# Two products that take turns on the tiles of x, a later mean, and other expected waits in a planned mixing stage

## The chip, the core and the metric

The kernel runs on one core of a Trainium2 chip. The metric is the device time of one execution in microseconds (us). Five engines run their own lists of instructions in order and wait for each other by semaphores: TensorE (PE, matmuls; its weight loads are listed as PEld), VectorE (DVE), ScalarE (ACT), GpSimd (POOL) and SyncE (SP, which issues nearly all transfers from HBM).

## The reference, cut to what matters

Two transformer blocks in float32 on 512 tokens of width 1024. The change lies in the first half of the first block. `x` is normalised, multiplied by `w_in`, and the columns of the product go to four groups of heads:

```python
def rms_norm(x, g):
    y = xf * lax.rsqrt(jnp.mean(xf * xf, axis=-1, keepdims=True) + EPS)
    return (y * g.astype(jnp.float32)).astype(x.dtype)

def token_mix(h, w_in, ...):
    p = (h @ w_in).astype(jnp.float32)
    ...                                   # fox attention: q, k, v, forget gates
    qkv = jax.nn.silu(causal_dwconv(gdn_qkv, gdn_conv_w))
    g = (-jnp.exp(gdn_a_log) * jax.nn.softplus(gdn_a + gdn_dt_bias)).transpose(0, 2, 1)
    o_b = gated_delta_chunked(l2norm(q), l2norm(k), v, g, beta)
    ...                                   # hgrn and gla: two more linear attentions
```

Then `x = x + mixed @ w_out`, a gated feed-forward with a convolution, and the second block (a convolution mixer, a feed-forward, latent attention, a feed-forward). Those parts are the same before and after.

## The kernel before, in words

**Products.** Everything is kept transposed, 128 features on the partitions and 512 tokens along the row. A product of `w_in` gives 128 output columns: eight k tiles, and for each three matmuls of 512 columns, because both operands are split in a high and a low part (`h` with `xh`, `h` with `xl`, `l` with `xh`; lines 705 ff., `step`). So a product is 24 matmuls into one bank of PSUM. These are the dense matmuls, `mm<-xh,wh`, `mm<-xl,wh`, `mm<-xh,wl` in the trace. The weights come from HBM into `raw` (ring of 3), ACT makes the high part `wh` (line 111) and DVE the low part `wl` (line 112); `wh` and `wl` are rings of 2, so the third weight tile can be split only when the first product is done with its own.

**The norm is late.** The products use `x` times the gain (`xh` line 173, `xl` line 174) without 1/rms. The sum of squares is made beside them (ACT squares, line 156, DVE adds, line 158, result `z`), one matmul with ones (`gps<-z,ones`) sums over the partitions, and `rsqrt_wide` (lines 131 to 146) makes `rb`, 1/rms. Whatever leaves a product's PSUM bank is multiplied with `rb` on the way, so no bank is freed before `rb` is there.

**What follows a product.** `sm` (small gates) is transposed, then ACT makes a softplus of it (`gtmp`, `gl`: Abs, Exp, Ln of lines 873 to 875 of the kernel before), four small DVE operations make `gg`, and a small matmul `gps<-gg,...` its cumulative sums. `gq`, `gk`, `gv` go through a convolution of four taps on ACT and DVE and a silu on ACT; the silu needs another activation table, which is loaded before it, and the table with Exp and Ln after it (1.28 us each).

**Order.** In this stage PE's order is written by a planner, `conduct`: it keeps a clock that advances with each matmul, three lanes of generators (G: the mean, the small gates, the delta rule `gdn0` and `gdn1`; L: `hg0`, `gla`, `hg1`; F: `fox0`, `fox1`) and the dense products as filler. A generator yields the wait it expects for the other engines (`Y_...`, `LV`, `LA`), and until the clock reaches that, PE's list is filled with dense steps. The tags of PSUM are `mm` (2 banks), `gps`, `lps` and `fps` (2 each). The order on the other engines is set by the compiler's scheduler. `start` issues the first loads and splits, `mean` yields `Y_MEAN`, then emits the matmul with ones.

Of the kernel before, what the change touches and what calls it, by code (L numbers as in the profile page):

```python
# [9 lines left out]
F32 = mybir.dt.float32  # L10
F32R = mybir.dt.float32r
# [4 lines left out]
ALU = mybir.AluOpType  # L16
# [11 lines left out]
class Builder:  # L28
# [19 lines left out]

    lane = {}

    def t(self, shape=(128, S), dt=F32, tag="t", bufs=None, name=None):
# [57 lines left out]
    def split(self, src, h, l, eng=None):  # L109
        nc = self.nc  # L110
        nc.scalar.activation(out=h, in_=src, func=ACTF.Copy)  # L111
        (eng or nc.vector).tensor_tensor(out=l, in0=src, in1=h.bitcast(F32), op=ALU.subtract)  # L112

# [16 lines left out]

    def rsqrt_wide(self, ps, scale, tag, n=S):

        nc = self.nc
        r = self.t(tag="u", bufs=3)[:, :n]
        nc.scalar.activation(out=r, in_=ps, func=ACTF.Ln, scale=scale, bias=self.epsD)
        v = self.t(tag="s", bufs=3)[:, :n]
        nc.scalar.activation(out=r, in_=r, func=ACTF.Exp, scale=-0.5)
        if n < S:
            nc.vector.tensor_scalar(out=v, in0=ps, scalar1=scale, scalar2=EPS, op0=ALU.mult, op1=ALU.add)
        else:  # L140
            nc.scalar.activation(out=v, in_=ps, func=ACTF.Identity, scale=scale, bias=self.epsD)
        nc.vector.tensor_tensor(out=v, in0=v, in1=r, op=ALU.mult)
        nc.vector.scalar_tensor_tensor(out=v, in0=v, scalar=-0.5, in1=r, op0=ALU.mult, op1=ALU.mult)
        out = self.t(tag=tag, bufs=3 if tag == "u" else 1) if tag else v
        nc.vector.scalar_tensor_tensor(out=out, in0=v, scalar=1.5, in1=r, op0=ALU.add, op1=ALU.mult)
        return out
# [505 lines left out]
Y_FIN, Y_FOX, Y_GDN, Y_SM = 8.3, 8.64, 4.0, 5.33  # L652
Y_MEAN = 9.5
C_MEAN = 4.2
C_SILU = 4.8
DUE = 4.78

# [6 lines left out]
class Mix(Mla):  # L664
# [93 lines left out]
    def conduct(self, jobs, lanes):  # L758


        self.clk = fed = 0.0
        started = 0
        self.over, self.beside = {None}, []
        self.there = ready = {}
        self.zs = []
        strands = [None] * len(lanes)
        first, last = jobs.pop(0), []
        self.last = last
        xs = [(k, *x) for k, x in enumerate(self.xs)]
        nxt, dense, held = (first, self.first), [], []  # L770
        early = [self.second]
        outs, parked, row = list(range(KD)), [], None
        while True:
# [13 lines left out]
            if nxt is None:  # L787
                job = next((j for j in jobs if j[1] in self.over), None)
                if job:
                    jobs.remove(job)  # L790
                    nxt = job, early.pop() if early else self.weight(self.a["w_in"], job[0], KD)
                elif not jobs and outs:
                    c = outs.pop(0)
                    nxt = (c, None, None, self.out_post(c)), self.weight(self.a["w_out"], c, KD)
# [29 lines left out]
            taken = [d[2] for d in dense] + [p[2] for p in parked] + ["mm"] * len(held)  # L824
            tag = next((t for t in tags if taken.count(t) < 2), None)
            if nxt and tag and len(dense) + len(held) < 2 and all(d[1][2] is None for d in dense):
                job, ws = nxt
                started += 1
                if started in (3, 4):
                    tag = "fps"  # L830
                dense.append((self.stepped(ws, last if job[2] is None else xs, tag), job, tag))
                nxt = None
                continue
# [202 lines left out]
    def gdn(self, p):  # L1036
# [36 lines left out]
        nc.vector.tensor_tensor(out=nk, in0=ss[:, 8:16], in1=rr[:, 8:16], op=ALU.mult)  # L1073
        yield 0.0
        MT, MR, AT, X, XT = [], [], [], [], []
        for j in range(2):
# [35 lines left out]
            MT.append(mt), MR.append(mr), AT.append(at), XT.append(xt)  # L1112
            yield LV
        nc.gpsimd.tensor_tensor(out=d4(ke), in0=d4(ko), in1=b64(eG), op=ALU.mult)
# [382 lines left out]
    def start(self, gi):  # L1497


        idle = self.psm.tile([128, S], F32, tag="lps", name="lps", bufs=2)  # L1500
        for _ in range(11):
            self.nc.tensor.matmul(out=idle[:, :128], lhsT=self.ones, rhs=self.ones, start=True, stop=True)
        self.x = [self.rt("x") for _ in range(KD)]
        self.first = self.weight(self.a["w_in"], T_SMALL, KD, lambda i: self.load(slice(0, 2)) if i else None)
        self.load(slice(2, KD))
        self.xs = self.norm(gi)
        self.second = self.weight(self.a["w_in"], TILES[ORDER.split()[1][:3]], KD)
        self.acc = self.squares(self.x, self.nc.vector)

    def load(self, ks):  # L1510
        for k in range(KD)[ks]:
            self.nc.sync.dma_start(out=self.x[k], in_=self.a["xT"][k])

    def mean(self):

        yield Y_MEAN
        ps = self.pst()
        self.mm(ps, self.ones, self.acc)
        with self.tc.high_priority():
            self.r = self.rsqrt_wide(ps, 1.0 / D, "rb")  # L1520

# [178 lines left out]
```

## Time and profile before

| | us |
|---|---|
| median of 3 runs (1855.84 to 1869.3) | 1856.73 |
| the profiled execution | 1857.77 |
| its span in the trace | 1856.0 |
| PE busy in the span | 1820.7 (98%) |
| DVE, ACT, POOL busy | 1053.8, 737.1, 197.2 |
| PE on the chain that ended last | 86% |

The trace is of the profiled execution; its clock and the run's differ by 1.77 us around the span. Read the share of PE first: where an engine is busy 98% of the time, what is left to look for is the stretches in which it is idle, or in which the granted clock (PEclk) is half of full speed. Then look for what ended each idle time. The names in the rows are those of the program's tiles; "out<-in".

### The profile page before, as it was taken

The page shows a single profiled execution, that of the slowest core. Times are in us where ns is not written, and L with a number is a line of the kernel's source. Part 1 is how long each engine was busy: PE and PEld are TensorE (multiplying, and loading weights), DVE is VectorE, ACT ScalarE, POOL GpSimd, SP SyncE. Part 2 cuts the span into 40 slices and gives each one's busy share as a digit, 9 for nine tenths or more (in the row PEclk, how much of TensorE's full clock was granted, in tenths as well). Part 3 has the DMA queues.
Part 4 walks back from the last instruction along what each step waited for, and adds up shares of the span by engine and source line. Part 5 has one row for each costly group of instructions (what it writes and reads, how often), then busy time and mean ns, then how long its engine had stood idle before and what let it go on. Part 6 is the DMA issues. An engine that isn't in the chain of part 4 may idle for free.

```text
span 1856.0 us, 22094 instructions
## 1 busy us (share of the span) xinstructions
PE 1820.7 (98%) x8631; PEld 1504.2 (81%) x8631; DVE 1053.8 (57%) x1622; ACT 737.1 (40%) x1138; POOL 197.2 (11%) x230
## 2 busy tenths in 40 slices
PE   9999999999999999999999999999999999999997
PEld 6788888778888888888888888888787888888886
DVE  7885976767777633455564444333876454444323
ACT  6543535554444422322342323323577333232322
POOL 2411402210000001111200000010011200000001
PEclk9999999999999999999999999999999999999999
DMA  5111111323222333232323232333212232323332
GB/s 177 48 35 47 46 35 35 120 88 102 92 101 96 92 94 99 97 102 91 103 96 101 93 98 96 94 95 101 69 57 75 80 102 92 103 91 100 94 94 77
DMA packets 53223, 162.61 MB, mean 88 GB/s; under 512 B 6528, under 2 KB 13184, under 8 KB 53120
## 3 DMA queue, kind: packets, MB, share of 16 engines
q1 hardware_dynamic: 52992, 161.21, 27.3%
q8 instruction: 67, 1.10, 0.2%
q14 instruction: 36, 0.29, 0.1%
q10 hardware_dynamic: 128, 0.01, 0.0%
HBM read 157.78 MB, written 2.10 MB: 86 GB/s over the span
## 4 chain that ended last, share of the span: by engine, by line
PE 86%; DVE 8%; ACT 3%; issue 1%; POOL 1%; DMA 0%; DVEq 0%; SPq 0%; POOLq 0%; ACTq 0%
PE mm L125 24%; PE mm L127 24%; PE mm L126 24%; PE mm L705 7%; PE gps L705 3%; PE lps L705 2%; PE fps L705 1%; DVE lbd L1317 1%; DVE wl L112 1%; DVE lat L1368 1%; ACT wh L111 1%; PE ps L577 0%; DVE ptl L112 0%; PE ps L165 0%; DVE nm L580 0%
## 5 line engine op out<-in xcount | busy, mean ns | idle before, releaser
L111 ACT ACTIVATE wh<-raw 128x1024 fp32r<-128x1024 f32 (+3 forms) x308 | 308.6, 1003 | 768.5 <-PE mm L126 459.1
L125 PE MATMUL mm<-xh,wh 128*128 128x512 f32 x1336 | 521.8, 391 | 0.5 <-ACT xh L173 0.5
L126 PE MATMUL mm<-xl,wh 128*128 128x512 f32 x1336 | 520.7, 390 | 0.5 <-DVE xl L174 0.5
L127 PE MATMUL mm<-xh,wl 128*128 128x512 f32 x1336 | 519.9, 389 | 0.0
L112 DVE TENSOR_TENSOR wl<-raw,wh 128x1024 fp32r<-128x1024 f32 (+3 forms) x300 | 362.9, 1210 | 225.6 <-ACT wh L111 222.7
L126 PEld LDWEIGHTS mm<-xl,wh 128*128 128x128 f32 x1336 | 250.8, 188 | 54.5 <-DVE xl L174 1.4
L125 PEld LDWEIGHTS mm<-xh,wh 128*128 128x128 f32 x1336 | 250.8, 188 | 53.8 <-issue 1.0
L127 PEld LDWEIGHTS mm<-xh,wl 128*128 128x128 f32 x1336 | 250.8, 188 | 52.1 <-issue 0.2
L125 PE MATMUL mm<-hidh,wh 128*128 128x512 f32 (+1 forms) x614 | 236.7, 386 | 0.0
L127 PE MATMUL mm<-hidh,wl 128*128 128x512 f32 (+1 forms) x614 | 235.3, 384 | 0.0
L126 PE MATMUL mm<-hidl,wh 128*128 128x512 f32 (+1 forms) x614 | 233.8, 381 | 0.0
L127 PEld LDWEIGHTS mm<-hidh,wl 128*128 128x128 f32 x614 | 115.4, 188 | 24.4
L126 PEld LDWEIGHTS mm<-hidl,wh 128*128 128x128 f32 x614 | 115.4, 188 | 23.6
L125 PEld LDWEIGHTS mm<-hidh,wh 128*128 128x128 f32 x614 | 115.5, 188 | 21.7 <-ACT wh L111 0.2
L705 PE MATMUL mm<-xh,wh 128*128 128x512 f32 x291 | 126.8, 436 | 0.5 <-ACT xh L173 0.4
L705 PE MATMUL mm<-xl,wh 128*128 128x512 f32 x291 | 115.4, 397 | 1.6 <-DVE xl L174 1.3
L705 PE MATMUL mm<-xh,wl 128*128 128x512 f32 x291 | 115.3, 396 | 1.5 <-DVE wl L112 1.5
L278 DVE TENSOR_TENSOR u<-mm,rb 128x512 f32<-128x512 f32 x44 | 30.4, 691 | 141.0 <-PE mm L127 141.0
L158 POOL TENSOR_TENSOR z<-z,sq 128x512 f32<-128x512 f32 x31 | 50.4, 1625 | 557.2 <-ACT sq L156 519.5
L274 DVE TENSOR_TENSOR u<-mm,rb 128x512 f32<-128x512 f32 x44 | 30.4, 691 | 90.9 <-PE mm L127 90.9
L111 ACT ACTIVATE hidh<-s 128x512 fp32r<-128x512 f32 x66 | 41.7, 632 | 88.4 <-DVE s L255 57.5
L215 DVE TENSOR_TENSOR x<-x,mm 128x512 f32<-128x512 f32 x32 | 22.0, 687 | 84.2 <-PE mm L127 84.2
(436 smaller groups left out, 2131.6 us busy)
## 6 DMA issues: line engine op xcount, KB each, us to landing
raw<-in_w_a_dram SPq DMA_DIRECT2D x52, 512.0 KB, 3.3
raw<-in_w_b_dram SPq DMA_DIRECT2D x52, 512.0 KB, 3.3
raw<-in_w_up_dram SPq DMA_DIRECT2D x44, 512.0 KB, 3.3
raw<-in_w_in_dram SPq DMA_DIRECT2D x28, 512.0 KB, 3.3
raw<-in_conv_w_in_dram SPq DMA_DIRECT2D x24, 512.0 KB, 3.3
raw<-in_w_down_dram SPq DMA_DIRECT2D x16, 448.0 KB, 3.4
raw<-in_w_a_dram SPq DMA_DIRECT2D x16, 448.0 KB, 3.4
raw<-in_w_b_dram SPq DMA_DIRECT2D x16, 448.0 KB, 3.4
```

What stands on the lines that cost most here:

```text
L111: nc.scalar.activation(out=h, in_=src, func=ACTF.Copy)
L112: (eng or nc.vector).tensor_tensor(out=l, in0=src, in1=h.bitcast(F32), op=ALU.subtract)
L125: nc.tensor.matmul(out=ps, lhsT=h, rhs=xh, start=(k == 0), stop=False)
L126: nc.tensor.matmul(out=ps, lhsT=h, rhs=xl, start=False, stop=False)
L127: nc.tensor.matmul(out=ps, lhsT=l, rhs=xh, start=False, stop=(k == kt - 1))
L158: eng.tensor_tensor(out=acc, in0=acc, in1=sq, op=ALU.add)
L215: self.nc.vector.tensor_tensor(out=self.x[c], in0=self.x[c], in1=ps, op=ALU.add)
L274: nc.vector.tensor_tensor(out=g, in0=ps, in1=r, op=ALU.mult)
L278: nc.vector.tensor_tensor(out=g, in0=ps, in1=r, op=ALU.mult)
L705: self.nc.tensor.matmul(out=out, lhsT=lhsT, rhs=rhs, start=start, stop=stop)
L1317: nc.vector.tensor_tensor(out=bd[rows, :, h].rearrange("p c (n j) -> p c n j", j=b), in0=c4(q)[rows], in1=c4(d)[rows], op=ALU.mult)
L1368: nc.vector.copy_predicated(out=at.rearrange("p c (n j) -> p c n j", j=2 * b)[:, :, :, b:], mask=self.lmask[:, lv - 1].rearrange("p (n j) ...
```

## The change

1. `start`: the first weight tiles of the first two products (`sm` and `gq`) are loaded and split in halves, with x's tiles between them. The two products then take turns: after two k tiles of the first and two of the second, each further tile of x is used by both before the next. Before, the first product ran alone, its weights in two halves, and the second product's weights came as one tile.
2. `conduct`: the third and fourth product go to the `fps` banks, and before the mean four products may stand in PSUM (`room`). `Y_MEAN` is 12.3 and counts from the end of the first two products; before it was 9.5 from the start.
3. `rsqrt_wide(..., short=True)` for this mean: the product with 1/D and the addition of EPS go from ACT to DVE, and the next weight tile's low part on DVE is held back until `rb` is made.
4. The delta rule: `Y_ROW` = 2.66 instead of 0 before the decay rows, and 2.5 LV instead of LV after the first of the two heads.

```diff
     def split(self, src, h, l, eng=None):
         nc = self.nc
         nc.scalar.activation(out=h, in_=src, func=ACTF.Copy)
-        (eng or nc.vector).tensor_tensor(out=l, in0=src, in1=h.bitcast(F32), op=ALU.subtract)
+        with ExitStack() as order:
+            if self.first_low is not None:
+                order.enter_context(self.tc.issue_after(self.first_low))
+                self.first_low = None
+            (eng or nc.vector).tensor_tensor(out=l, in0=src, in1=h.bitcast(F32), op=ALU.subtract)
...
-        if n < S:
+        if n < S or short:
             nc.vector.tensor_scalar(out=v, in0=ps, scalar1=scale, scalar2=EPS, op0=ALU.mult, op1=ALU.add)
         else:
             nc.scalar.activation(out=v, in_=ps, func=ACTF.Identity, scale=scale, bias=self.epsD)
...
-        nc.vector.scalar_tensor_tensor(out=out, in0=v, scalar=1.5, in1=r, op0=ALU.add, op1=ALU.mult)
+        i = nc.vector.scalar_tensor_tensor(out=out, in0=v, scalar=1.5, in1=r, op0=ALU.add, op1=ALU.mult)
+        if short:
+            self.first_low = i.ins
...
-Y_MEAN = 9.5
-C_MEAN = 4.2
+Y_MEAN = 12.3
+C_MEAN = 4.0
 C_SILU = 4.8
+Y_ROW = 2.66
...
-        started = 0
+        started = 2
...
-        first, last = jobs.pop(0), []
+        last = []
...
-        nxt, dense, held = (first, self.first), [], []
-        early = [self.second]
+        nxt, dense, held = None, [], []
+
+        two = [(self.stepped(ws, xs, "mm"), jobs.pop(0)) for ws in self.firsts]
+        for i in (0, 0, 1, 1, *(0, 1) * (KD - 2)):
+            ps, k = next(two[i][0])
+            if k == KD - 1:
+                held.append((ps, *two[i][1][2:]))
...
-            tag = next((t for t in tags if taken.count(t) < 2), None)
-            if nxt and tag and len(dense) + len(held) < 2 and all(d[1][2] is None for d in dense):
+            tag = "fps" if started in (2, 3) else next((t for t in tags if taken.count(t) < 2), None)
+            room = 2 if "mean" in self.over else 4
+            if nxt and tag and len(dense) + len(held) < room and all(d[1][2] is None for d in dense):
                 job, ws = nxt
                 started += 1
-                if started in (3, 4):
-                    tag = "fps"
...
         nc.vector.tensor_tensor(out=nk, in0=ss[:, 8:16], in1=rr[:, 8:16], op=ALU.mult)
-        yield 0.0
+        yield Y_ROW
...
             MT.append(mt), MR.append(mr), AT.append(at), XT.append(xt)
-            yield LV
+            yield LV if j else 2.5 * LV
...
-        self.first = self.weight(self.a["w_in"], T_SMALL, KD, lambda i: self.load(slice(0, 2)) if i else None)
-        self.load(slice(2, KD))
-        self.xs = self.norm(gi)
-        self.second = self.weight(self.a["w_in"], TILES[ORDER.split()[1][:3]], KD)
+        steps = (("w", 0, 0), ("x", 0), ("x", 1), ("w", 1, 0), ("x", 2), ("x", 3), ("w", 0, 1), ("x", 4),
+                 ("w", 1, 1), ("x", 5), ("x", 6), ("x", 7))
...
         with self.tc.high_priority():
-            self.r = self.rsqrt_wide(ps, 1.0 / D, "rb")
+            self.r = self.rsqrt_wide(ps, 1.0 / D, "rb", short=True)
```

What this does to the lists of instructions is seen at three places. The number behind a tile's name is its buffer.

PE, around the matmul of the mean. Before, in the middle of the second product (`mm_281`, `gq`); the third (`mm_333`, `gk`) goes to another tag's bank:

```order
L705 MATMUL mm_281<-xh_156,wl_167 128x512
L705 MATMUL gps_303<-z_170,ones_77 128x512 [waits DVE_49]
L705 MATMUL mm_281<-xh_160,wh_166 128x512
L705 MATMUL mm_281<-xl_161,wh_166 128x512
L705 MATMUL mm_281<-xh_160,wl_167 128x512
L705 MATMUL mm_333<-xh_132,wh_277 128x512 [waits Activation_49]
L705 MATMUL mm_333<-xl_133,wh_277 128x512
L705 MATMUL mm_333<-xh_132,wl_278 128x512 [waits DVE_49]
```

Now, behind the last matmul of the fourth product (`mm_343`, `gv`); next is the fifth (`mm_415`, `lq`):

```order
L715 MATMUL mm_343<-xl_167,wh_308 128x512
L715 MATMUL mm_343<-xh_166,wl_309 128x512
L715 MATMUL gps_368<-z_170,ones_77 128x512
L715 MATMUL mm_415<-xh_132,wh_339 128x512 [waits DVE_49,Activation_49]
L715 MATMUL mm_415<-xl_133,wh_339 128x512
```

Before, 45 dense matmuls stood ahead of the mean and a product that needs no `rb` behind it; now 96 stand ahead of it, and the product behind it takes the bank of `sm`, so it waits for DVE as well as for ACT.

DVE, from the making of `rb` to what leaves the first two banks. Before (L142, L143, L145 are the three steps to `rb`; L901 takes `sm` out of its bank):

```order
L142 TENSOR_TENSOR u_307<-u_307,u_305 128x512 [waits Activation_49]
L143 SCALAR_TENSOR_TENSOR u_307<-u_307,u_305 128x512 [waits DVE_49]
L112 TENSOR_TENSOR wl_330<-raw_327,wh_329 128x1024 [waits DMAHW5_49,PE_49,Activation_49]
L145 SCALAR_TENSOR_TENSOR rb_312<-u_307,u_305 128x512 [waits DVE_49]
L901 TENSOR_TENSOR sm_314<-mm_250,rb_312 128x512 [waits DVE_49]
```

Now:

```order
L146 TENSOR_SCALAR u_372<-gps_368 128x512 [waits Activation_49]
L149 TENSOR_TENSOR u_372<-u_372,u_370 128x512 [waits DVE_49,Activation_49]
L150 SCALAR_TENSOR_TENSOR u_372<-u_372,u_370 128x512 [waits DVE_49]
L152 SCALAR_TENSOR_TENSOR rb_377<-u_372,u_370 128x512 [waits DVE_49]
L118 TENSOR_TENSOR wl_412<-raw_409,wh_411 128x1024 [waits DMAHW0_49,PE_49]
L915 TENSOR_TENSOR sm_379<-mm_250,rb_377 128x512 [waits DVE_49]
```

The weight split has moved from ahead of the last step to behind it, and still stands ahead of `sm`; a step that ACT did is now the first row.

ACT, around the softplus of the small gates (`gtmp`, `gl`). Before, it stands ahead of all silus:

```order
L226 ACTIVATE gq_322<-z_319,mixp_222 128x512 [waits DVE_49,Pool_49]
L873 ACTIVATE gtmp_375<-gz_371 128x32 [waits DVE_49]
L873 ACTIVATE u_388<-u_387 4x512
L874 ACTIVATE gtmp_375<-gtmp_375 128x32 [waits Activation_49]
L874 ACTIVATE u_388<-u_388 4x512 [waits Activation_49]
L875 ACTIVATE gl_374<-gtmp_375 128x32 [waits Activation_49]
```

Now (line 270 loads the silu's table, line 273 the other; `wh_523` is the weight tile that takes the sixth product's buffer):

```order
L887 ACTIVATE gtmp_453<-gz_449 128x32 [waits DVE_49]
L1452 DMA fk_938<-sm_379 1x16x32 [waits DVE_49]
L888 ACTIVATE gtmp_453<-gtmp_453 128x32 [waits Activation_49]
L113 ACTIVATE wh_523<-raw_521 128x1024 [waits DMAHW2_49,PE_49]
L270 ACT_TABLE_LOAD
L270 ACTIVATE gv_400<-gv_400 128x512 [waits DVE_49]
L270 ACTIVATE gk_392<-gk_392 128x512
L270 ACTIVATE gq_384<-gq_384 128x512
L273 ACT_TABLE_LOAD
L889 ACTIVATE gl_452<-gtmp_453 128x32 [waits Activation_49]
```

The last step, `gl`, has moved behind a weight split that waits for PE, two table loads and three silus. On PE the matmul of `gg`, which needs it, stands three dense matmuls behind the end of the sixth product; the transposes of `gk` and `gq`, which stood 45 dense matmuls behind it, follow at once, and fifteen dense matmuls come between them and the decay rows, where there were none.

## Rows read from the trace of the kernel before

**Rows 1.** The page, busy time of each engine, its share and instructions.

```profile
PE 1820.7 (98%) x8631; PEld 1504.2 (81%) x8631; DVE 1053.8 (57%) x1622; ACT 737.1 (40%) x1138; POOL 197.2 (11%) x230
```

**Rows 2.** PE in order of time: start, length, operation, count, [idle before, releaser].

```profile
6.36 0.49 PE L705 MATMUL mm<-xh,wh 128*128 128x512 f32 x1 [0.25 <-ACT xh L173]
...
9.06 0.40 PE L705 MATMUL mm<-xh,wl 128*128 128x512 f32 x1
...
17.44 0.50 PE L705 MATMUL mm<-xh,wl 128*128 128x512 f32 x1 [1.50 <-DVE wl L112]
...
21.89 1.02 PE L705 MATMUL gps<-z,ones 128*128 128x512 f32 x2
...
36.21 0.40 PE L705 MATMUL mm<-xl,wh 128*128 128x512 f32 x1
...
46.01 0.39 PE L705 MATMUL mm<-xh,wl 128*128 128x512 f32 x1
47.65 0.66 PE L712 MATMUL gps<-mlac,gk 128*128 128x128 f32 x4 [1.25 <-ACT gk L261]
48.17 0.66 PE L712 MATMUL gps<-mlac,gq 128*128 128x128 f32 x4
...
51.65 0.59 PE L705 MATMUL gps<-mixb,identb 128*128 128x512 bf16 x1 [2.82 <-issue]
```

**Rows 3.** Stretches: length, busy time of PE, PEld, DVE, ACT, POOL, granted clock, DMA.

```profile
50.00:51.00 1.00, 0.00 (x0) 0.00 (x0) 0.43 (x1) 1.00 (x4) 0.00 (x0) 0.71 0.00 0
...
57.00:58.00 1.00, 1.00 (x5) 0.77 (x5) 1.00 (x6) 0.59 (x3) 0.03 (x1) 0.88 0.88 291
...
230.00:240.00 10.00, 8.01 (x34) 6.65 (x33) 7.77 (x18) 2.79 (x3) 0.53 (x1) 0.74 0.15 54
240.00:250.00 10.00, 10.00 (x54) 8.70 (x53) 6.21 (x15) 1.06 (x1) 0.53 (x1) 0.92 0.00 0
...
290.00:300.00 10.00, 9.07 (x48) 7.61 (x49) 8.52 (x15) 8.15 (x17) 7.56 (x7) 0.83 0.16 55
```

**Rows 4.** DVE in order of time, 12 to 40 us.

```profile
12.38 2.10 DVE L174 SCALAR_TENSOR_TENSOR xl<-x,gains,xh 128x512 fp32r<-128x512 f32 x3
...
17.31 2.69 DVE L158 TENSOR_TENSOR z<-z,sq 128x512 f32<-128x512 f32 x3
...
26.11 1.22 DVE L112 TENSOR_TENSOR wl<-raw,wh 128x1024 fp32r<-128x1024 f32 x1
...
27.96 0.69 DVE L901 TENSOR_TENSOR sm<-mm,rb 128x512 f32<-128x512 f32 x1
...
38.46 0.74 DVE L228 SCALAR_TENSOR_TENSOR gk<-z,mixp,gk 128x512 f32<-128x512 f32 x1
```

**Rows 5.** ACT in order of time, 20 to 50 us.

```profile
21.10 1.04 ACT L111 ACTIVATE wh<-raw 128x1024 fp32r<-128x1024 f32 x1
22.05 0.19 ACT L1242 ACTIVATE lb<-lb 128x2 f32<-128x2 f32 x1
22.95 0.69 ACT L135 ACTIVATE u<-gps,epsD 128x512 f32<-128x512 f32 x1 [0.72 <-PE gps L705]
...
24.11 0.63 ACT L137 ACTIVATE u<-u 128x512 f32<-128x512 f32 x1
...
46.98 0.61 ACT L261 ACTIVATE gk<-gk 128x512 f32<-128x512 f32 x1
...
48.13 1.28 ACT L264 ACT_TABLE_LOAD   x1
```

**Rows 6.** PE's waits from 50 to 430 us: total, times, longest.

```profile
PE lps L705 <- DVE lst L1408: 2.1, 2, 1.3
PE lps L705 <- DVE gate L1022: 2.0, 1, 2.0
...
PE gps L705 <- DVE gxt L1146: 0.6, 1, 0.6
...
PE gps L705 <- DVE gx L1143: 0.5, 1, 0.5
```

More of the change, by code (lines that the diff above doesn't have):

```diff
@@ L49 @@
     lane = {}
+    first_low = None
     def t(self, shape=(128, S), dt=F32, tag="t", bufs=None, name=None):
@@ L128, in product, with rsqrt_wide @@
         return ps
-    def rsqrt_wide(self, ps, scale, tag, n=S):
+    def rsqrt_wide(self, ps, scale, tag, n=S, short=False):
         nc = self.nc
@@ L790, in conduct @@
                     jobs.remove(job)
-                    nxt = job, early.pop() if early else self.weight(self.a["w_in"], job[0], KD)
+                    nxt = job, self.weight(self.a["w_in"], job[0], KD)
                 elif not jobs and outs:
@@ L1502, in start @@
             self.nc.tensor.matmul(out=idle[:, :128], lhsT=self.ones, rhs=self.ones, start=True, stop=True)
+        nc = self.nc
         self.x = [self.rt("x") for _ in range(KD)]
-        self.first = self.weight(self.a["w_in"], T_SMALL, KD, lambda i: self.load(slice(0, 2)) if i else None)
-        self.load(slice(2, KD))
-        self.xs = self.norm(gi)
-        self.second = self.weight(self.a["w_in"], TILES[ORDER.split()[1][:3]], KD)
[L1508 to L1512, printed above, removed]
+        cts = T_SMALL, TILES[ORDER.split()[1][:3]]
+        raw = [self.raw.tile([128, CHUNK * 128], F32, tag="raw", name="raw") for _ in cts]
+        h = [self.wh.tile([128, CHUNK * 128], F32R, tag="wh", name="wh") for _ in cts]
+        l = [self.wl.tile([128, CHUNK * 128], F32R, tag="wl", name="wl") for _ in cts]
+        steps = (("w", 0, 0), ("x", 0), ("x", 1), ("w", 1, 0), ("x", 2), ("x", 3), ("w", 0, 1), ("x", 4),
+                 ("w", 1, 1), ("x", 5), ("x", 6), ("x", 7))
+        half = lambda i: slice(i * 512, i * 512 + 512)
+        for what, i, *part in steps:
+            if what == "x":
+                nc.sync.dma_start(out=self.x[i], in_=self.a["xT"][i])
+            else:
+                cs = half(part[0])
+                nc.sync.dma_start(out=raw[i][:, cs], in_=self.a["w_in"][cts[i], :, cs])
+        self.xs = []
+        for what, i, *part in steps:
+            if what == "x":
+                self.xs.append(self.gained(self.x[i], self.gain(gi, i), "x"))
+            else:
+                cs = half(part[0])
+                self.split(raw[i][:, cs], h[i][:, cs], l[i][:, cs])
+        col = lambda t, k: t[:, k * 128 : (k + 1) * 128]
+        self.firsts = [[(col(h[i], k), col(l[i], k)) for k in range(KD)] for i in range(2)]
+        self.acc = self.squares(self.x, nc.vector)
     def mean(self):
```

## The prediction

> **What bounds the kernel now.** I read the busy times first: PE is busy 98% of the span [rows 1]. No other engine is over 57%. So the time is PE's list, and a change can win or lose only where PE issues nothing, or runs at half clock. Next I read PE in order of time through the first 60 us, the only place where the change moves whole products, and the granted clock beside it. A dense matmul issues every 0.228 us: 43 of them lie between 36.21 and 46.01 [rows 2]. Everything below counts PE time that is lost against that pace, up to the first `gps<-gq,gk` matmul of the delta rule. What PE has to issue is otherwise the same; the 15 dense matmuls that the change puts ahead of that point are missing later.
>
> Lost before, four pieces. (1) Start: the first dense matmul is at 6.36, the mean's at 21.89, and the 45 between are worth 10.3, so 5.2 lost, 1.5 of it one wait for a weight's low part at 17.44 [rows 2]. (2) From the end of the seventh product (46.01 + 0.23) to the transposes of `gk` at 47.65: 1.4, ended by ACT's silu [rows 2]. (3) From the end of `gq`'s transposes (48.17 + 0.5) to the decay rows at 51.65: 3.0 [rows 2]. (4) Clock: mean 0.71 in 50 to 51 and 0.88 in 57 to 58 [rows 3] put the fall to half speed (1.2 instead of 2.4 GHz) at 50.4 and the return at 57.2; PE works again from 51.65, so 5.6 us at half speed, 2.8 lost. Sum 12.4.
>
> **The change, part by part.**
>
> *Taking turns.* The first six matmuls go as before, since the same three transfers stand ahead of them: they end at 9.06 + 0.23, 2.9 us for 1.4 of work, 1.5 lost [rows 2]. After that each tile of x gives six matmuls, 1.4 us, while DVE needs 0.7 for its low part (three in 2.10) [rows 4] and half as much again for the weight halves. The next 42 should run without a gap, to 18.9. SP's list counts as nothing: 20 transfers of the same bytes stand ahead of the third weight tile in both kernels, and the last three tiles of x come behind the other halves, by at most what PE is behind them anyway. POOL's list doesn't change here.
>
> *The third product.* Both `wh` buffers are now in use until 18.7, so its split can't be early. On ACT it stands behind the three small `lb` steps, which follow DVE's adds of squares. Before, these adds ended at 20.0 (17.31 + 2.69) [rows 4], the third `lb` step began 2.05 later with one 1.04 split between [rows 5], and DVE's work up to there is the same now. At worst the split ends at 22.1, at best, without `lb` ahead, at 19.8. Then two matmuls, and 0.8 more until the low part (1.22) [rows 4] is there. Lost between 1.7 and 4.0; I take 3.4, near the row with `lb` ahead. The early gain is given back here.
>
> *The mean.* Before, the chain from its matmul at 21.89 to `sm` out of its bank at 28.65 took 6.8 us [rows 2, 4], and PE felt nothing: 27 dense matmuls that needed no 1/rms covered it. That is the point: the third product didn't wait for 1/rms before either. Now the mean comes when all four products are done, and the fifth needs `sm`'s bank. The chain itself gets shorter: Ln ended at 23.64 and Exp began at 24.11, and the 0.5 of Identity between goes [rows 5]; the weight split on DVE only moves from ahead of the last step to a place that is still ahead of `sm`, so it saves nothing; ACT has a 1.04 split [rows 5] that starts with the mean's matmul and ends about when Ln may begin, 0.1 more. So 6.4, less 0.5 for the mean's own issue (two passes in 1.02) [rows 2]: 5.9 lost. If that split holds Ln up whole it is 6.9; without the DVE split, 4.8.
>
> *The small gates.* On PE the matmul of `gg` stands three dense matmuls behind the sixth product's end. On ACT the last step to it stands behind `wh_523`, which needs that product's end. From there: split 1.04, table 1.28, three silus 1.7 (the last two took 48.13 - 46.98 = 1.15), table 1.28, Ln 0.2 (as the small `lb` step) [rows 5], four small DVE steps at about the same, partly overlapped, 0.6, and 0.2 for the last matmul to end. That is 6.3, less 0.7 for the three matmuls: 5.6 lost. It holds however early or late the sixth product ends. This rests on ACT not passing a waiting instruction. The trace shows it: `gk`'s last tap ended at 39.2 on DVE [rows 4], and its silu ran at 46.98 [rows 5] behind other work. The Trainium skill, "TensorE: Matmul & The Clock Gate" (Architectural detail), says the same, that ACT and DVE are strict first-in first-out while PE alone may pull weight loads ahead. Were the Ln free to pass, this term and its clock below would go and the sum would end 8.4 lower.
>
> *The waits ahead of the delta rule.* Pieces (2) and (3) of before go: `gk` and `gq` have been through the silu by then, and 15 dense matmuls (3.4 us) cover the 3.0.
>
> *Clock.* Nearly 6 us without a matmul twice; before, 2.0 us idle at 232.7 was enough for a fall. A fall cost 2.8 in (4), and elsewhere 6.8 us at half speed (clock 0.74 and 0.92 in 230 to 250), 3.4 lost, or 3.4 us (0.83 in 290 to 300), 1.7 lost [rows 3]. I take 2.8 each, the row nearest in kind, between 1.7 and 3.4. The skill's same page (What's actually happening) says that the gate's time base runs free of the kernel's start; by that each fall's cost would be drawn anew in each run, anywhere between the two bounds.
>
> *Longer waits later.* What the delta rule itself kept waiting after that point is 0.6 and 0.5 us [rows 6], and the fall of the clock near 290 that follows them, 1.7. The longer expected waits aim at these: 2.8 gained. The other waits are the linear attention's (`lps`), which get no new wait; I leave them.
>
> **Sum.** Lost after: 1.5 + 3.4 + 5.9 + 5.6 + 2 x 2.8 = 22.0; before 12.4; so 9.6 slower there, less 2.8 later: 6.8. The profiled execution took 1857.77, so 1864.6. It lies 1.04 above the median of the runs shown, so **1864** in their terms (1863.5).
>
> **Rivals.**
>
> *Not slower: the later lanes gain more.* The largest wait later is `gate` 2.0 [rows 6] with the fall at 234.7 behind it, 3.4 [rows 3]; DVE is what it waits for, and the second delta rule now no longer runs beside that part of the linear attention. With the two `lst` waits (2.1) [rows 6] gone as well, 7.5 more comes back: 1856. It decides if PE's idle time after 100 us falls below half of before. For it: the change moves work out of that stretch. Against it: the same work then lies beside `hg1`, and waits of one place tend to come back in another. Chance 0.22.
>
> *Slower still.* The wait for the third product's weights is itself long enough for a fall of the clock (2.8 more), and the pattern of the small gates, a weight split that waits for PE with tables and silus behind it, recurs once in front of the second delta rule (5.6): 1872. For it: 2.0 idle was enough once; against it: 1.5 idle at 17.44 was not. Chance 0.15.
>
> *The change doesn't do what its order says.* If the small gates' value is there early enough, or the mean's chain is covered after all, one of the long waits with its clock (8.4) is missing: 1855. Only the places in the lists speak against it, but these are fixed. Chance 0.08.
>
> *The forecast*: two new long waits of PE, 1859 to 1869. Chance 0.55.
>
> **Numbers.** The range for 8 in 10 is 1853 to 1873: the forecast with its bounds, most of the two cheaper cases and the middle of the dearer one. A measurement of this kernel can tell about 1% from no change, 18.6 us. Faster than 1838 would need nearly all of PE's idle time in the stage back: 0.02. Slower than 1875 needs the dear case and more: 0.06. Within 1%: 0.92.
>
> **What would show it.** In PE's list of the changed kernel: a wait of about 3 us for `wh` at the third product; 5 to 7 us between the mean and the fifth product, ended by DVE's `sm`; 5 to 6 us ahead of `gg`, ended by DVE after ACT's second table load; half clock behind each; no wait at the decay rows. The prediction is wrong in its main step if the idle time ahead of the fifth product is under 3 us, wrong in its second if `gg` isn't waited for, and wrong in what is left if the waits after 100 us shrink by more than 6 us or grow.

## The result, and the profile after

The changed kernel takes **1879.3 us** (median of 6 runs, 1877.87 to 1880.63) against 1856.8 before: ratio 1.011, with an interval of 1.0083 to 1.0137. It is slower by 22, where 7 were forecast, and 6 above the end of the range. The profiled execution took 1877.87; its span is 20.1 longer than that of before.

All of it is lost in the stage that the change touches. This is the line of the stage that comes next, the first helper call behind the mixing; its column "first and last start" gives the time at which the next stage begins.

```profile
L131 PE MATMUL mm<-xh,wh x151: 388/390/792, 415.2 to 519.6; 128*128 128x512 f32 x151
```

Before, the same line starts at 395.0, so 20.2 are gone by then; from there to the end both kernels take 1461 us. So each kernel below has two marks: the first `gps<-gq,gk` of the delta rule (60.27 before, 73.80 after), up to which the forecast counted, and this one.

PE in order of time up to the first mark (start, length, operation, idle time before it and what ended it), to be set beside [rows 2]:

```profile
5.95 0.50 PE L715 MATMUL mm<-xh,wh 128*128 128x512 f32 x1 [0.56 <-ACT xh L182]
...
21.33 0.64 PE L715 MATMUL mm<-xh,wh 128*128 128x512 f32 x1 [3.19 <-ACT wh L113]
...
34.26 1.02 PE L715 MATMUL gps<-z,ones 128*128 128x512 f32 x2
40.86 0.77 PE L715 MATMUL mm<-xh,wh 128*128 128x512 f32 x1 [5.58 <-DVE sm L915]
...
60.78 0.61 PE L715 MATMUL gps<-gg,mixc 128*128 128x16 f32 x2 [5.48 <-DVE gg L980]
...
68.04 0.39 PE L715 MATMUL gps<-mixb,identb 128*128 128x512 bf16 x1
...
73.80 1.16 PE L715 MATMUL gps<-gq,gk 64*128 64x128 f32 x8
```

The three waits stand where the forecast put them, and the decay rows (68.04) wait for nothing. Up to here the change costs 73.80 - 60.27, less 15 dense matmuls (3.4) and four small transposes (0.5) that now stand ahead of this point: 9.6.

The other 10.6 come behind it. Between the two marks PE's idle time grew from 9.7 to 17.4, and its time at half clock from 10.2 to 13.7, which is 1.7 lost at most. These are 9.4 of the 10.6; the rest isn't placed. PE's seven largest waits from 80 to 480 us (total, times, longest):

```profile
PE fps L715 <- ACT fpt L1496: 6.4, 2, 4.0
PE mm L715 <- ACT xh L113: 2.3, 2, 1.5
PE gps L722 <- DVE u L1021: 1.9, 1, 1.9
PE gps L715 <- ACT gvn L1191: 1.6, 1, 1.6
PE fps L715 <- ACT sq L1456: 1.3, 1, 1.3
PE lps L715 <- DVE lat L1382: 1.3, 1, 1.3
PE lps L715 <- DVE lst L1422: 0.7, 1, 0.7
```

Against [rows 6]: `gate` (2.0) is gone, `lst` is down from 2.1, and in their place stands `fpt`, the transposed softmax weights of the fox lane, for which no wait is listed before. Stretches with the granted clock (columns as in [rows 3]):

```profile
20.00:30.00 10.00, 8.48 (x30) 6.40 (x31) 2.96 (x7) 3.29 (x5) 0.00 (x0) 0.83 0.33 107
40.00:50.00 10.00, 9.14 (x33) 7.41 (x34) 8.54 (x15) 4.68 (x7) 0.20 (x2) 0.73 0.15 52
60.00:70.00 10.00, 9.21 (x40) 7.94 (x41) 7.32 (x25) 6.96 (x19) 1.05 (x1) 0.70 0.01 2
270.00:280.00 10.00, 6.03 (x29) 4.94 (x28) 5.30 (x17) 6.65 (x16) 0.00 (x0) 0.83 0.16 52
300.00:310.00 10.00, 7.53 (x32) 5.96 (x31) 6.50 (x12) 7.42 (x14) 4.66 (x5) 0.74 0.15 52
310.00:320.00 10.00, 10.00 (x66) 8.78 (x64) 3.42 (x8) 2.29 (x5) 0.00 (x0) 0.92 0.01 2
370.00:380.00 10.00, 8.27 (x38) 6.67 (x37) 4.96 (x9) 3.92 (x7) 0.31 (x1) 0.83 0.43 116
```

A lower clock follows each wait of about 2 us or more: the third product's weights (20:30), the mean, `gg`, both waits on `fpt`, and those on `u` (1.88) and `xh` (1.51) at 370. Why `fpt` is late shows in ACT's list ahead of it, in order of time:

```profile
268.65 1.06 ACT L113 ACTIVATE wh<-raw 128x1024 fp32r<-128x1024 f32 x1
269.73 1.28 ACT L270 ACT_TABLE_LOAD   x1
271.02 1.15 ACT L270 ACTIVATE gate<-gate 128x512 f32<-128x512 f32 x2
272.19 1.28 ACT L273 ACT_TABLE_LOAD   x1
...
274.17 0.27 ACT L1496 ACTIVATE fpt<-fps 128x128 f32<-128x128 f32 x1
```

PE's transpose that fills its bank ran here, and the product that needs the copy here:

```profile
268.78 0.27 PE L722 MATMUL fps<-mlac,fp 128*128 128x128 f32 x1
...
274.49 0.69 PE L715 MATMUL fps<-fv,fpt 128*128 128x64 f32 x2 [3.97 <-ACT fpt L1496]
```

The input is ready at 269.05, 0.4 after ACT has begun a weight split. ACT then does split, table load, two silus and table load, 4.8 us, and three small steps, 0.7, before it gets to a copy of 0.27. The second wait has the same pattern ahead of it, with one silu:

```profile
300.37 1.04 ACT L113 ACTIVATE wh<-raw 128x1024 fp32r<-128x1024 f32 x1
...
303.37 1.28 ACT L273 ACT_TABLE_LOAD   x1
304.67 0.49 ACT L1496 ACTIVATE fpt<-fps 128x384 f32<-128x384 f32 x1
305.21 1.54 PE L715 MATMUL fps<-fv,fpt 128*128 128x64 f32 x6 [2.47 <-ACT fpt L1496]
```

The pattern alone isn't enough. The kernel before has it once too (split at 291.34, table load, two silus, table load, copy), and there PE doesn't wait, since eight `gps<-gx,gmt` and three dense matmuls stand ahead of the product that needs the copy:

```profile
294.87 1.28 ACT L264 ACT_TABLE_LOAD   x1
296.16 0.49 ACT L1482 ACTIVATE fpt<-fps 128x384 f32<-128x384 f32 x1
297.14 0.78 PE L705 MATMUL fps<-fv,fpt 128*128 128x64 f32 x6
```

So it takes both, a copy that is late on ACT and a place in PE's list with nothing left to do.

### The profile page after: what moved, and what is told of

The parts are those of the page before. It is cut to its first block, busy times and chain, and to the rows that moved or that the text cites. A ratio compares the mean times of both kernels' runs of the same rounds, so it can differ in the third digit from the quotient of the medians.

```text
span 1876.1 us, 22127 instructions
## 1 busy us (share of the span) xinstructions
PE 1824.9 (97%) x8631; PEld 1509.4 (80%) x8631; DVE 1055.9 (56%) x1624; ACT 740.0 (39%) x1138; POOL 194.2 (10%) x230
## 4 chain that ended last, share of the span: by engine, by line
PE 87%; DVE 6%; ACT 4%; issue 1%; POOL 1%; DMA 0%; SPq 0%; DVEq 0%; ACTq 0%; POOLq 0%
PE mm L131 24%; PE mm L133 24%; PE mm L132 24%; PE mm L715 9%; PE gps L715 2%; PE lps L715 2%; PE fps L715 1%; ACT wh L113 1%; DVE lat L1382 1%; DVE wl L118 1%; POOL s L1320 0%; PE ps L586 0%; PE ps L174 0%; DVE ptl L118 0%; DVE nm L589 0%
## 5 line engine op out<-in xcount | busy, mean ns | idle before, releaser
L118 DVE TENSOR_TENSOR wl<-raw,wh 128x1024 fp32r<-128x1024 f32 (+4 forms) x301 | 366.2, 1217 | 231.2 <-ACT wh L113 228.3
L131 PEld LDWEIGHTS mm<-xh,wh 128*128 128x128 f32 x1336 | 251.0, 188 | 53.4 <-issue 1.0
L715 PEld LDWEIGHTS mm<-xh,wh 128*128 128x128 f32 x292 | 57.4, 197 | 25.0 <-issue 8.5
```

The costliest lines, as they stand in the source:

```text
L131: nc.tensor.matmul(out=ps, lhsT=h, rhs=xh, start=(k == 0), stop=False)
L715: self.nc.tensor.matmul(out=out, lhsT=lhsT, rhs=rhs, start=start, stop=stop)
```

## The experiments

Of each, the marks and the last two columns are of the profiled execution; the ratio is to runs of the kernel before on the same chip (medians 1856.8 to 1857.6). In brackets stand the dense matmuls ahead of the first mark, 0.23 us each, since the marks of two kernels compare only at equal work. The last two columns are PE's idle time and its time at half clock (granted clock 0.5) between the marks, in us. delta_only, mean_5_2 and placebo_fox were profiled in an execution well above their median (1888.2, 1894.5, 1876.5), so their second mark and last column don't fit the median beside them.

| kernel | median us | ratio (95%) | first `gq,gk` | next stage | idle | half clock |
|---|---|---|---|---|---|---|
| before | 1856.8 | | 60.27 (165) | 395.0 | 9.7 | 10.2 |
| after | 1879.3 | 1.0083 to 1.0137 | 73.80 (180) | 415.2 | 17.4 | 13.7 |
| delta_only | 1868.5 | 1.0035 to 1.0085 | 57.30 (180) | 424.7 | 18.2 | 68.3 |
| start_only | 1869.3 | 1.0048 to 1.0096 | 72.02 (168) | 404.9 | 9.0 | 10.2 |
| mean_5_2 | 1880.2 | 1.0077 to 1.0167 | 65.06 (177) | 431.1 | 17.3 | 61.4 |
| warm_mean | 1874.6 | 1.0075 to 1.0146 | 70.46 (180) | 409.8 | 17.1 | 10.2 |
| row_only | 1877.3 | 1.0099 to 1.0129 | 57.34 (180) | 409.9 | 23.2 | 23.9 |
| lv_only | 1865.4 | 1.0033 to 1.0062 | 59.64 (165) | 399.6 | 15.1 | 6.8 |
| no_lv | 1898.0 | 1.0195 to 1.0228 | 73.38 (180) | 436.4 | 22.2 | 47.8 |
| mean52_row | 1881.6 | 1.0126 to 1.0154 | 65.19 (177) | 419.6 | 20.9 | 34.1 |
| swap_wait | 1855.8 | 0.9982 to 0.9999 | 55.56 (168) | 392.4 | 12.6 | 10.2 |
| fpt_on_dve | 1883.0 | 1.0103 to 1.0145 | 74.89 (180) | 420.0 | 15.5 | 27.3 |
| mean52_start | 1876.1 | 1.0084 to 1.0112 | 63.01 (162) | 406.5 | 18.4 | 6.8 |
| nosilu_before | 1852.1 | 0.9943 to 0.9986 | 54.17 (165) | 388.4 | 9.3 | 10.2 |
| nosilu_after | 1865.3 | 1.0025 to 1.0052 | 67.02 (180) | 402.3 | 12.6 | 10.2 |
| placebo_gdn | 1866.2 | 1.0028 to 1.0058 | 58.62 (165) | 401.7 | 14.1 | 17.1 |
| placebo_fox | 1863.8 | 1.0020 to 1.0060 | 58.51 (165) | 413.3 | 16.7 | 37.5 |

My theory after seeing the trace was that the two longer waits in the delta rule cost the late time; the rival, that the new start did it.

**The two halves of the change apart.**

```diff
 delta_only: before, with
-        yield 0.0
+        yield 2.66
-            yield LV
+            yield LV if j else 2.5 * LV
 start_only: after, with both of these lines as before
```

> The kernel before with the two longer waits in the delta rule and nothing else (2.66 ahead of the decay rows, 2.5 LV after the first head). Theory A, the late loss of some 10 us in the changed kernel comes from these waits, which push the second delta rule and the fox lane against other work: 15 dense matmuls cover the wait at the decay rows and the half clock behind it (5.8 us won), 10 lost later, so about 1861. Theory B, the late loss comes from the start's delay and the new order there: about 1851, with no PE wait over 2.5 us after 100 us.

> The changed kernel without the two longer waits in the delta rule. In both theories the waits of 5.6 us ahead of the fifth product and 5.5 us ahead of the small gates' matmul stay, and the wait at the decay rows comes back, since no dense matmuls stand there (about 3 us and part of a half-clock stretch). Theory A: the late loss of 10 goes, so about 1873. Theory B: it stays, so 1882 or more.

Each half alone costs 11 to 12 us. delta_only's first mark is 3.0 earlier, with 15 dense matmuls more ahead of it, since the decay rows' wait is covered. Then it has the late waits of the whole change (`u` 1.9 and `gvn` 1.6 too), beside one of its own on `gmt` (2.0), and comes out at 1868.5 where theory A had 1861:

```profile
PE fps L705 <- ACT fpt L1482: 6.5, 2, 4.0
PE mm L705 <- ACT xh L111: 2.3, 2, 1.5
```

start_only keeps the three early waits, and no wait on `fpt` stands in it; behind the first mark it is idle for 9.0, where the kernel before has 9.7, so it loses nothing late. Of the wait at the decay rows 0.4 came back and not 3. So on either of these starts the late waits come with the delta rule's edits.

**The mean's wait.** The mean of squares 21 matmuls earlier, so that the fifth product has them as cover; or 13 idle matmuls behind it, which keep PE at work and cover nothing.

```diff
 mean_5_2: after, with
-Y_MEAN = 12.3
+Y_MEAN = 5.2
 warm_mean: after, with, behind the mean's matmul,
+        for _ in range(13):
+            self.nc.tensor.matmul(out=idle[:, :128], lhsT=self.ones, rhs=self.ones, start=True, stop=True)
```

> The changed kernel with Y_MEAN 5.2 instead of 12.3: the mean's matmul stands behind 75 dense matmuls, not 96, so 21 of the fourth product cover the chain to 1/rms, and the compiler puts the small gates' Ln ahead of the silus again. If the two long waits with their half-clock stretches are the early loss (5.6 + 5.5 + two times 2.8), 16 us come back: about 1863 if the late loss stays, about 1853 if it was a consequence. If the early loss has another cause (the taking turns, the halves), no more than 5 come back: 1874 or more.

> The changed kernel with 13 matmuls of ones with ones behind the mean's matmul, which nobody reads; they fill most of the 5.6 us in which PE waits for the fifth product's bank. The wait itself stays. If the half clock behind it costs 2.8 us, the fifth product starts at full clock and the kernel is 2 to 3 us faster, about 1876.5; if a fall of the clock costs next to nothing, 1879 to 1880. The compiler also puts the small gates' Ln ahead of the silus here; since the transposes of gk, which follow at once, need the silus, I expect the wait of 5.5 to move there and not to shrink by more than 1.

In mean_5_2 the waits on `sm` and on `gg` go, a wait of 4.0 on `gk`'s silu comes in, and the first mark is 8.7 earlier, not 16. Its runs lie in two groups, 1870 to 1871 and 1889 to 1894. The trace is of the upper one and has a stretch of some 51 us at half clock behind the second wait on `fpt`; that the lower group keeps the gain for want of such a stretch is inferred. warm_mean's lower runs (1872 to 1875, four of six) are 5 to 7 us under the changed kernel, with the mean's chain no shorter. In its trace the fifth product starts at full clock, and the first mark is 3.3 earlier: that much is the clock behind the mean's wait and a shorter wait on `gg` (3.3 for 5.5), as ACT's list came out in another order there. Another 2.1 come behind the mark, where it has 10.2 us at half clock for 13.7.

**The two delta edits apart, on either start.**

```diff
 row_only: before, with
-        yield 0.0
+        yield 2.66
 lv_only: before, with
-            yield LV
+            yield LV if j else 2.5 * LV
 no_lv: after, with
-            yield LV if j else 2.5 * LV
+            yield LV
 mean52_row: no_lv with Y_MEAN = 5.2
```

> The kernel before, with the one added expected wait of 2.66 between the decay rows and the delta rule; the 2.5 times longer steps and the new start are left out. Theory (the late loss comes from the 2.5 times longer steps, which shift the later parts of the delta rule against the fox lane): the wait of 2.4 us on the decay rows at 55 us and the stretch of lower clock behind it go (2.8), no wait of 2 us or more on fpt appears: 1857.6 - 5.2 = about 1852 us. Rival (any shift of the delta rule by 2 to 3 us sets the other lanes out of step): fpt waits of 2.5 to 4 us appear here too and the time is 1862 to 1868 us.

> The kernel before, with only the 2.5 times longer expected wait after the first half of the delta rule's matrices. Theory (this is the edit that costs the late time): the decay-row wait stays, two fpt waits of 2.5 to 4 us with lower clock behind them appear, 1866 to 1872 us. Rival (the two added waits cost it only together): no fpt wait of 2 us, 1855 to 1860 us.

> The changed kernel without the 2.5 times longer steps: new start and the wait of 2.66 before the delta rule. Theory (the 2.5 times longer steps carry the late loss): the same as the new start alone, 1866 to 1870 us, with the waits on sm (5.6), gg (5.5) and wh (3.2) and none of 2 us on fpt. Rival (the shift by the 2.66 costs as much): 1876 to 1880 us, with fpt waits of 2.5 to 4 us.

> The changed kernel without the 2.5 times longer steps, and with the mean of squares put 21 matmuls earlier (expected wait 5.2 for 12.3), so that its wait has 24 matmuls of cover and more of the third and fourth product behind it. Theory (the change loses by the three uncovered waits at the start and by the late waits of the longer steps): the wait on sm and the one on gg go, the wait on wh (3.2 with its clock 1.5) and one on the gates (4) stay, none on fpt: 1857.6 - 5.2 + 3.2 + 1.5 + 4 = about 1861 us. Rival (late loss comes with any new order of the start): 1869 to 1872 us with fpt waits.

My theory fell here. The edit that covers the decay rows costs 20 us by itself (row_only), although the first mark is 2.9 earlier; the 2.5 times longer step costs 8; both together on the same start 11. On the new start, row_only's edit without the other gives 1898, 29 above start_only; in its trace PE is idle for 13.2 more between the marks, and at half clock for 37.6 more, 27 of them in one stretch behind a wait of 2.94 on `fp` that ended at 139.88. mean52_row came out at 1881.6, above both the theory's 1861 and the rival's 1869 to 1872, with 5.2 on `fpt` in one wait. What an edit costs is no property of the edit. The late waits in row_only are others than in delta_only: `gate` 3.9 in two, `gat` 3.6, `rq` 2.6, `fp` 2.1.

The next theory: each edit moves the delta rule against the fox and attention lanes, all three share ACT and DVE, and any new order lets other instructions fall together.

**The cover without the shift; the copy on another engine; the start without the delta edits.** In swap_wait the first delta rule's step on the decay rows comes later by 2.66 and the wait behind it is shorter by as much, so that the steps after it keep about their places (PE's list differs from that of before only within a stretch of some 250 rows behind the transposes of `gk`, and at one place later). fpt_on_dve has PE's list of the changed kernel, row for row.

```diff
 swap_wait: before, with
-        yield 0.0
+        yield 0.0 if p else 2.66
-            yield Y_GDN / (1 + j)
+            yield Y_GDN / (1 + j) - (2.66 if p == j == 0 else 0.0)
 fpt_on_dve: after, with
-            nc.scalar.activation(out=pt[:, :n], in_=tp[:, :n], func=ACTF.Copy)
+            nc.vector.tensor_copy(out=pt[:, :n], in_=tp[:, :n])
 mean52_start: start_only with Y_MEAN = 5.2
```

> The kernel before; in the first delta rule alone, the expected wait of 2.66 is put ahead of the decay rows' step, and the wait behind that step is cut from 4.0 to 1.34, so that the products behind it stand where they stood. Theory (covering the decay rows is worth its own wait of 2.8 and the lower clock behind it, and what row_only lost comes from the new order of everything behind): 1857 - 5.6 = 1851 to 1853 us, with 40:60 at full clock. Rival (the exponentials then come 2.66 later, and their products wait instead): the wait of 2.8 comes back on gat or gmt, 1856 to 1858 us or more.

> The changed kernel with one edit: the transposed softmax weights (fpt) are copied out of PSUM by VectorE instead of ScalarE; TensorE's order is the same row for row. Theory (fpt is late because its copy stands on ScalarE behind a weight split, two table loads and a silu): both fpt waits (6.4 together) and the lower clock behind them (3.7 more than before in 260:400) go, 1879 - 9 = about 1870 us. Rival (ScalarE's next work for the lane, the exponential fp, stands behind the same loads, or VectorE is as full): the wait turns up on fp, sm or gvn and the time stays at 1876 to 1880 us.

> The changed kernel's start alone (neither of the two longer waits in the delta rule), with the mean of squares 21 matmuls earlier (expected wait 5.2). Theory (the start alone loses by its uncovered waits on sm and gg, and its own order does no harm later): start_only 1869 less the waits on sm (5.6) and gg (5.1) and 3 of clock, plus a wait of 4 on the gates gk: 1858 to 1861 us, no fpt wait of 2 us. Rival (each new order brings late waits): 1866 us or more with new waits of 2 us or more between 80 and 400 us.

Behind 80 us swap_wait has only waits that the kernel before has too, which is the theory's part, and of the kernels that leave nothing out it is the one that beats both, if the one before by 1.2 us only (ratio 0.999, no more than just clear of 1). The gain isn't the 5.6 expected, and the rival says why. PE, in order of time (the decay rows at 52.27 wait for nothing):

```profile
72.07 0.66 PE L712 MATMUL gps<-mlac,gv 128*128 128x128 f32 x4 [1.37 <-DVE gat L1031]
...
78.53 1.08 PE L712 MATMUL gps<-mlac,gxt 128*128 128x128 f32 x4 [2.58 <-DVE gxt L1111]
```

and DVE's step that ends the last wait:

```profile
76.75 1.64 DVE L1111 TENSOR_TENSOR gxt<-u,mlac 128x512 fp32r<-128x512 f32 x1
```

PE is 4.7 ahead at `gq,gk` and gives 4.0 of it back in two new waits. DVE hands out the second `gxt` at 78.39; in the kernel before it did so at 78.06, with the wait at the decay rows. That wait of PE was time that DVE's chain needed anyway. A fall of the clock follows here as well (0.92 in 80 to 90).

In fpt_on_dve the late `fpt` waits are gone, but one of 1.83 appears in the first fox lane, where DVE is the fuller engine (busy 7.6 and 8.0 of 10 in 120 to 140, ACT 6.5 and 4.0), and others later (`gx` 2.1). It came out 4 us slower where 9 were to be gained (one of its five runs, 1873.5, is 6 faster). PE's idle time between the marks did shrink, from 17.4 to 15.5, but the time at half clock there doubled, from 13.7 to 27.3, half of it behind the wait of 1.83 (last section).

In mean52_start the first mark is 9.0 earlier than in start_only and the kernel 7 us slower, with new waits between 80 and 480 (`gko` 2.3, `lw` 2.1, `fpt` 1.9) that start_only hasn't. The rival of that run again.

**Two causes told apart, and two edits that have nothing to do with the change.** The first pair leaves the silus of the mixing stage out in both kernels, without moving a row on PE. The second pair shifts one lane of the kernel before a little.

```diff
 nosilu_before, nosilu_after: in before and in after,
-                ins = self.silu(y, y, i == n - 1)
+                ins = self.nc.scalar.activation(out=y, in_=y, func=ACTF.Copy).ins
 placebo_gdn, placebo_fox: before, with Y_GDN = 4.5 (was 4.0); before, with Y_FOX = 10.0 (was 8.64)
```

> The kernel before with the silus of the mixing stage left out (plain copies of the same size stand in their place), and with them their table loads; TensorE's order is the same row for row. It is the control of nosilu_after. Theory (table loads end only short waits here: gk 1.3, gate 2.0 in part): 1857 - 2 to 5 = 1852 to 1855 us. Rival (ScalarE is covered wherever the order was set for it): 1856 to 1858 us.

> The changed kernel with the silus of the mixing stage left out in the same way; TensorE's order is the same row for row. Theory (the waits on gg and on fpt are those of copies and small sums that stand on ScalarE behind silus and table loads): gg falls from 5.5 to 3 or less, both fpt waits (6.4) to under 1 each and the clock behind them stays up, 1879 - 2.5 - 5 - 5 = about 1867 us. Rival (the late waits come from the order on TensorE and VectorE, whatever ScalarE does): fpt stays above 3 in all and the time at 1875 us or more.

> The kernel before, with one expected wait of the delta rule's step changed from 4.0 to 4.5 units; nothing of the change is in it. Theory (the order of before is one that fits, and any shift of a lane behind 60 us lets others fall together, which costs 5 to 20 us): 1862 to 1877 us, with new waits of 2 us or more. Rival (only the waits that the change edits do harm): 1855 to 1859 us.

> The kernel before, with the fox lane's first expected wait changed from 8.64 to 10.0 units; nothing of the change is in it, and its delta rule stands as it did. Theory (any shift of one lane against the others costs): 1862 to 1877 us. Rival (only a shift of the delta rule does harm): 1855 to 1859 us.

All four came out as the theories had them, except that one wait on `fpt` stayed at 1.1. Without silus and table loads the changed kernel is 14.0 faster, the kernel before 4.8. Up to the first mark both gain alike (6.8 and 6.1); behind it the changed kernel gains 6.1 and the kernel before 0.5. So of the 10.6 lost late, about 5.6 goes with the silus and their table loads, the clock behind their waits included. In nosilu_after, `gg` waits 0.18 (5.48 with silus); there ACT does the Ln of `gl` at 52.19, ahead of the weight split at 54.61, so this wait went by order as well as by length. Ahead of `fpt` ACT's order stayed, split and copies of the same size included, and the waits are

```profile
PE fps L715 <- ACT fpt L1496: 1.3, 2, 1.1
```

The two edits that belong to nothing cost 9 and 7 us, with 4.4 and 7.0 more of idle time between the marks. In placebo_fox it is `fpt` again,

```profile
PE fps L705 <- ACT fpt L1482: 3.9, 1, 3.9
```

and placebo_gdn, a shift of the delta rule, has nearly the late waits of lv_only, also a shift of the delta rule. In placebo_gdn `gate` stands at 4.2, `rq` at 2.6 and `lst` at 2.5, in lv_only at 3.8, 2.6 and 2.5.

## Why the prediction was wrong

- **Taking turns, the third product: right.** The first 48 matmuls end at 18.14 (21.33 less the wait of 3.19), 0.8 earlier than 18.9; the third product's wait was 3.19 for `wh` and 0.19 for `wl`, against 3.4, and the split did stand behind `lb` on ACT.
- **The mean: right.** 5.58 against 5.9, ended by DVE's `sm`.
- **The small gates: right.** 5.48 against 5.6, ended by DVE after ACT's second table load, behind split, table, three silus and table as forecast. In nosilu_after it is 0.18; since the Ln moved ahead of the split there, what the split alone costs isn't shown.
- **Clock: nearly right.** Two falls at 2.8 were counted. Both cost somewhat less, counted as in piece (4), from where PE works again to the return of full clock: the mean's 2.3 (0.73 in 40 to 50 puts the return at 45.4; PE works from 40.86), `gg`'s 2.6 (0.70 in 60 to 70: 66.0; from 60.78). The third product's wait brought one more (0.83 in 20 to 30, 3.4 us at half speed: 1.6), which had been put into a rival.
- **The sum to the first mark: right,** 9.6 against 9.6, in part by luck: 0.7 less at the start and 0.7 less for the two falls made up for the 1.6 of the third.
- **"Longer waits later: 2.8 gained; the other waits I leave them": this step failed.** It was 10.6 lost, and the prediction's own sign for it, waits behind that grow, came true (idle 9.7 to 17.4). What the step aimed at did happen: `gxt` and `gx` of the delta rule wait for nothing worth naming any more, and `gate` is gone. But the step looked only at the waits that the edit aims at. start_only, without the longer waits, has none of this loss. With them the delta rule moves against the fox and attention lanes, which share ACT and DVE with it; the copy of `fpt` fell twice behind weight split, table load, silu and table load where PE had no more cover, 6.4 us with a lower clock behind both. That pattern I had worked out myself, for `gg`, and had priced a second one in the rival "slower still" (5.6, put in front of the second delta rule; it came in the fox lane, twice). The rival got 0.15 and the case got it nearly whole. ACT's list of the changed kernel shows `fpt` behind the silus as it shows `gg`; I had read it only up to 60 us and in the delta rule. That list alone wouldn't have been enough: the kernel before has `fpt` behind them once, covered.
- **"Waits ahead of the delta rule go": right here, not by itself.** The decay rows don't wait any more, and in the changed kernel no wait on the delta rule's next steps follows up to 140 us. In the order of before, swap_wait shows that the same cover is worth 1.2 and not 5.6, since DVE ends the next step of the chain.
- **The rival "not slower"** counted on `gate` and `lst` coming back as time. They did shrink, and other waits took their place, as its own line against it had said. Its condition, idle time halved behind 100 us, is wrong by the waits above.
- **The chances.** Slower than 1875 had 0.06; it was 1879. The late part could go either way by 10 us, as the placebos (7 and 9 lost), row_only (20) and lv_only (8) show, and the range allowed for 5.6 and 2.8.

What stays open: about 5.0 of the 10.6 remain late without silus, spread over `xh` 2.3, `u` 1.9, a new 1.8 on `gmt` and others, and I haven't taken these apart. Parts 1 to 3 of the change were never run apart from each other; what each does is read from the trace.

## What to carry to other kernels

Where one engine's list is 98% full and others serve several lanes at once, an expected wait that is lengthened for one lane is an edit of all lanes: read every list of the helper engines behind it, and look in them for small copies behind table loads and behind steps that wait for the full engine, at places where the full engine's list has nothing between that doesn't need the copy. Cover for a wait is worth only what the next engine in that chain has left; follow the chain one step further before counting it. To learn what a shift of a schedule is worth, shift something unrelated by as little first: here two such shifts cost 7 and 9 us of 1857.

## What the runs showed of the hardware

What a wait of PE costs in clock isn't fixed by its length. After 3.97 us without a matmul the changed kernel had 0.83 in 270 to 280, which is 3.4 us at half speed; after its second wait on `fpt`, 2.47, it had 0.74 and 0.92 in 300 to 320, which is 6.8. After the same second wait, 2.49 long and ended at 292.87, delta_only's profiled execution stayed at half speed (1.2 of 2.4 GHz) for some 51 us (6.6 + 40 + 4.6), and mean_5_2's, also after 2.49, as long; the columns are length, busy time (matmuls), granted clock, DMA's share and GB/s:

```profile
290.00:300.00 10.00, 7.51 (x28) 0.67 0.15 52
300.00:320.00 20.00, 20.00 (x75) 0.50 0.02 4
320.00:340.00 20.00, 20.00 (x71) 0.50 0.07 23
340.00:350.00 10.00, 10.00 (x52) 0.77 0.42 133
```

After 1.83, ended at 140.24 (fpt_on_dve), it was some 14 us:

```profile
140.00:145.00 5.00, 4.76 (x22) 0.72 0.00 0
145.00:150.00 5.00, 5.00 (x19) 0.50 0.00 0
150.00:155.00 5.00, 5.00 (x19) 0.50 0.00 0
155.00:160.00 5.00, 5.00 (x32) 0.91 0.29 105
```

Behind these waits PE had work without a gap. The same kernel can come out either way: the eight runs of delta_only go from 1864.1, with a mean clock of 0.994, to 1888.2, with 0.979, four of them at 1864 to 1866. That the longer ones come from the long half-speed stretch is inferred from their mean clocks; only one of them has a trace. Two other kernels bear it out: mean_5_2 and placebo_fox, profiled in their longest execution, have stretches of 51 and 24 us at half speed, and warm_mean, profiled in its lower group, none over 6.8. So a wait of 2 us late in a stage carries a risk of 20 that one trace of the kernel need not show.
